# Hybrid attention, retention and state-space kernel on one core: mixers as parallel tasks, retention products ordered by shape, attention sums accumulated onto the scores

## The chip, the cores and the metric

The kernel runs on one core of a Trainium2 chip. The metric is the device time of one execution in microseconds (us). The core's engines are named as the profile names them: PE (TensorE, matrix products), PEld (its weight loads), DVE (VectorE), ACT (ScalarE), POOL (GpSimd) and SP (SyncE, which issues the DMAs here). Each engine takes its instructions in the order in which the built program lists them.

## The reference

Two layers over 528 positions (16 meta tokens and 512 inputs) of width 1024. Each layer projects the normed input to 23 blocks of 128 columns, feeds three mixers, multiplies their joined output by `w_out`, adds it to the stream, and ends with a gated MLP of width 2816. The three mixers:

```python
# stick-breaking attention, 6 heads, per block of 128 queries
z = einsum('bhqd,bhkd->bhqk', qb, kb) * scale
log1m = where(mask, log_sigmoid(-z), 0.0)
between = cumsum(log1m, axis=3, reverse=True) - log1m
w = where(mask, exp(log_sigmoid(z) + between), 0.0)
out = einsum('bhqk,bhkd->bhqd', w, vb)
# retention, 6 heads, chunks of 128: inside the chunk, and a state carried between chunks
scores = einsum('bhnid,bhnjd->bhnij', qc, kc) * decay_in
inner = einsum('bhnij,bhnje->bhnie', scores, vc)
o = inner + cross            # cross: the decayed state times q
# state space (S5): 16 groups, a complex diagonal recurrence, gelu, a gated product
```

## The kernel before

All matrix work in the large products is done as three products of split operands: a float is cut into a high part and a low part, and high times high, low times high and high times low are summed in PSUM (`mm3`, line 346). So each weight block needs a split on ACT (`wh`) and on DVE or POOL (`wl`), and each mixer output needs one too (`slow_split`, line 365: ACT writes `hi`, DVE or POOL writes `lo`). Products of 264 columns come in twos, since 528 positions fill two PSUM banks. The tiles `pj` are the results of the projections, of the gated product of S5, of the out product and of the MLP.

**How the order is made.** The program is written by a recorder. The projections are written one after the other, and between the products of `mm3` the function `tick` (line 183) lets waiting tasks write one step each. A task is a Python generator; `spawn` (line 166) adds it, and it goes on when its modelled time has come and what it asked for is there. Tasks share 5 PSUM banks (`banks`, `freed`, lines 177 and 180) and 7 attention groups. `drain` (line 200) writes tasks with no projection between them until a condition holds. The framework below then sorts the instructions of each engine once more by its own modelled times, keeping the dependencies. What reaches the chip is a fixed order for each engine.

**The mixers in the order before.** In each layer four lanes run beside the projections: two attention lanes (`sb_lane`, line 1094, one for each head of a pair, over three pairs), one retention lane (`ret_lane`, line 1105, three pairs one after the other) and one S5 lane (`s5_lane`, line 1112), which waits for both halves of `u`, runs `s5_mix` (line 702) over half 0 and then half 1, and then `s5_glu` (line 790). After the projections the out product is written in three parts (line 1142), each behind a `drain` for its mixers: attention, S5, retention in the first layer, and S5, attention, retention in the second.

**One attention group** (`sb_group`, line 816). Scores go into a bank `z` (products `z<-sq,sk`, with a mask product ahead of them in two of three groups). ACT makes log(1+exp(-|z|)) in tile `e` with three passes. DVE writes the softplus `sp` = max(z,0)+`e` and the log sigmoid `e` = min(z,0)-`e`, and the bank is given back. DVE then adds to `sp` the `sp` of the next block of keys, so that each block holds the running sum of all later ones. `sp` is split into `hi` (ACT) and `lo` (POOL). A second bank `s` takes the sums: products with `tri` (strict triangle) within a block and with `tric` (its complement) for the next block, 18 products with `tri` or `tric` for each head. DVE adds `s` to `e`, ACT takes the exponential, and the weights are split once more and multiplied with the values (`av`). Each head has three groups: A (432 columns), B2 (416) and B1 (512).

**One retention pair** (`ret_pair`, line 942). Transposes (`rtp`), a product for the states (`kv`), scores (`sc`) and then the output `ro`: for each of five chunks two products of 64 output rows, one per head, and one of 128 output rows with the state.

Of the kernel before, what the change touches and what calls it, by code (L numbers as in the profile page):

```python
# [9 lines left out]
F32R = mybir.dt.float32r  # L10
# [5 lines left out]
P = 128  # L16
# [20 lines left out]
Q = 4  # L37
# [51 lines left out]
def hybrid_kernel(ctx, tc, A, out, dbg=None):  # L89
# [137 lines left out]
    for name, g in (("A", G_A), ("B2", G_B2)):  # L227
# [3 lines left out]
        for j, q0, q1, o0 in g:  # L231
# [3 lines left out]
            if j == 4:  # L235
# [11 lines left out]
                    compare_op=ALU.is_gt, fill=0.0)  # L247
    G.affine_select(out=tri_f[:, P:2 * P], in_=tri_f[:, P:2 * P], pattern=[[1, P]], base=0, channel_multiplier=-1,
# [3 lines left out]
    tric = const([P, P], F32R, "tric")  # L252
    V.tensor_copy(out=tric, in_=tri_f[:, P:2 * P])
# [448 lines left out]
    def s5_mix(l, u, par, ys):  # L702
# [3 lines left out]
        for hf in range(2):  # L706
            ut = u[hf]
            uc = tt("uc")
            for t in range(4):
                for j in range(Q):  # L710
                    (SC.copy if (t + j) % 2 else V.tensor_copy)(
                        out=n3(uc)[32 * (3 - j):32 * (3 - j) + 32, t, :],
                        in_=ut[32 * t:32 * t + 32, :].rearrange("p (n q) -> p n q", q=Q)[:, :, j])
                yield
            pr, pi = ph[hf]
            fr, fi, y1, y2 = tt("fr"), tt("fi"), tt("y1"), tt("y2")
            for b in range(2):
                yield from banks(2)
                es = []
                for ri in range(2):  # L720
                    ps = bank("es")
                    for t in range(2):
                        mm(ps[:, NCH * t:NCH * t + NCH], lhsT=we[ri, hf][:, P * (2 * b + t):P * (2 * b + t) + P],
                           rhs=n3(uc)[:, 2 * b + t, :], start=True, stop=True)
                    es.append(ps)
                yield
                c = slice(HALF * b, HALF * b + HALF)
                er, ei = es[0][:, :HALF], es[1][:, :HALF]
                V.tensor_tensor(out=fr[:, c], in0=er, in1=pr[:, c], op=ALU.mult)
                V.tensor_tensor(out=y1[:, c], in0=ei, in1=pi[:, c], op=ALU.mult)  # L730
                V.tensor_tensor(out=fi[:, c], in0=ei, in1=pr[:, c], op=ALU.mult)
                V.tensor_tensor(out=y2[:, c], in0=er, in1=pi[:, c], op=ALU.mult)
                yield
                freed(2)
                G.tensor_tensor(out=fr[:, c], in0=fr[:, c], in1=y1[:, c], op=ALU.add)
                G.tensor_tensor(out=fi[:, c], in0=fi[:, c], in1=y2[:, c], op=ALU.subtract)
            yield
            for t in range(4):
                d0 = rho[:, 4 * hf + t:4 * hf + t + 1].to_broadcast([P, NCH])
                for z in (fr, fi):  # L740
                    V.tensor_tensor_scan(n3(z)[:, t, :], d0, n3(z)[:, t, :], 0.0, op0=ALU.mult, op1=ALU.add)
                if t % 2:
                    yield
            xr, xi, y2 = tt("xr"), tt("xi"), tt("y2")
            V.tensor_tensor(out=xr, in0=fr, in1=pr, op=ALU.mult)
            V.tensor_tensor(out=y1, in0=fi, in1=pi, op=ALU.mult)
            yield
            G.tensor_tensor(out=xr, in0=xr, in1=y1, op=ALU.subtract)
            V.tensor_tensor(out=xi, in0=fr, in1=pi, op=ALU.mult)
            V.tensor_tensor(out=y2, in0=fi, in1=pr, op=ALU.mult)  # L750
            yield
            G.tensor_tensor(out=xi, in0=xi, in1=y2, op=ALU.add)
            yield
            y = tt("ysm")
            for b in range(2):
                yield from banks(1)
                ps = bank("yps")
                for t in range(2):
                    o, tq = NCH * t, 2 * b + t
                    mm(ps[:, o:o + NCH], lhsT=tz[hf][:, P * tq:P * tq + P], rhs=n3(uc)[:, tq, :], start=True, stop=False)  # L760
                    for ri, x in ((0, xr), (1, xi)):
                        mm(ps[:, o + 1:o + NCH], lhsT=gg[ri, hf][:, 160 * tq + 32:160 * tq + 160],
                           rhs=n3(x)[:, tq, 0:NCH - 1], start=False, stop=ri == 1)
                yield
                for t in range(2):
                    tq = 2 * b + t
                    for i in range(Q):
                        V.scalar_tensor_tensor(
# [3 lines left out]
                            in1=ps[32 * i:32 * i + 32, NCH * t:NCH * t + NCH], op0=ALU.mult, op1=ALU.add)  # L772
                    yield
                freed(1)
            dump(f"ys{l}{hf}", y)

            y3 = tt("y3")
            SC.activation(y3, y, AF.Square)
# [505 lines left out]
```

## Time and profile before

| what | value |
|---|---|
| median of 3 runs | 1407.82 us (1406.98 to 1408.22) |
| the profiled execution | 1408.06 us, its span 1406.3 us |
| granted TensorE clock, mean over the span | 0.983 |
| PE busy | 97% of the span, 9020 products |
| DVE, ACT, POOL busy | 62%, 44%, 36% |
| DMA | 118.26 MB, mean 84 GB/s |

How to read the views. *Page, busy time*: an engine's busy us, share of the span, instructions. *Page, chain*: the work that ended last, followed back; shares of the span by engine. *Windows*: a stretch in us from the span's start, its length, then the busy us of PE, PEld, DVE, ACT and POOL, each with its instruction count, then the granted TensorE clock as a share of full speed (1.00 is 2.4 GHz, 0.50 is 1.2 GHz), the DMA share and GB/s; a window of PE alone has PE's busy time, the clock and the DMA columns. *Waits*: who waited for whom, us in total, times, longest. *Timeline*: start, duration, engine, line, operation, tiles, shape, count of merged instructions, and in brackets the idle time ahead and what ended it. *Lines*: group, shapes, count, then busy us and mean ns of one, then the idle time ahead. Products overlap in PE's pipeline: what one takes of PE is the distance from its start to the next start, not its duration. A float32 product (`ro`, `sc`, `kv`, `z`, `hps`) shows as two instructions in the trace.

### The profile page before, as it was taken

Reading aid. Unit: us, or ns where it says so; the run is one execution under the profiler, and the core shown is the slowest. Engines: PE = TensorE matmul, PEld = TensorE weight load, DVE = VectorE, ACT = ScalarE, POOL = GpSimd, SP = SyncE. Lnnn points to the kernel's source line nnn. Section 1 sums busy time; section 2 is a strip of 40 time slices with the busy share of each in tenths; the row PEclk is TensorE's granted clock in tenths of the full one; section 3 lists DMA queues with packets and bytes.
Section 4 is the critical chain, followed back from the end, with each engine's and each line's share of the span. In section 5 each row is a group of like instructions: output and inputs, shape, how many; then the busy total and the mean of one; then the engine's idle time right before and its main releaser. Section 6 shows DMA issues by size and latency. Waiting matters only on the chain. (4 is left out here: it accounts for less than half of the span.)

```text
span 1406.3 us, 22614 instructions
## 1 busy us (share of the span) xinstructions
PE 1362.0 (97%) x9020; PEld 1241.9 (88%) x9020; DVE 878.0 (62%) x1456; ACT 617.3 (44%) x1002; POOL 512.8 (36%) x625
## 2 busy tenths in 40 slices
PE   6999998899999999999999999999999999999998
PEld 6989888799989999999999898989788888888886
DVE  8897888768454645544556788774585543554453
ACT  4466475355343223322344565773363432442231
POOL 5686536322589402200223452653222210220020
PEclk9999899799999999999999999999999999999999
DMA  4212112113312222232232121222232322323223
GB/s 153 69 61 97 46 61 83 51 34 109 110 64 76 91 90 91 91 91 91 79 99 94 61 77 46 70 68 81 78 106 90 103 93 90 105 91 100 95 75 105
DMA packets 38985, 118.26 MB, mean 84 GB/s; under 512 B 4960, under 2 KB 5472, under 8 KB 38880
## 3 DMA queue, kind: packets, MB, share of 16 engines
q1 hardware_dynamic: 38880, 116.82, 25.6%
q8 instruction: 71, 1.16, 0.3%
q14 instruction: 34, 0.28, 0.1%
HBM read 111.46 MB, written 2.10 MB: 81 GB/s over the span
## 5 line engine op out<-in xcount | busy, mean ns | idle before, releaser
L131 PE MATMUL pj<-xh,wh 128*128 128x264 f32 (+1 forms) x1792 | 459.0, 312 | 16.7 <-ACT wh L121 5.3
L131 PE MATMUL pj<-xh,wl 128*128 128x264 f32 (+1 forms) x1792 | 456.3, 310 | 3.5 <-DVE wl L121 3.5
L131 PE MATMUL pj<-xl,wh 128*128 128x264 f32 (+1 forms) x1792 | 456.7, 311 | 1.8 <-DVE xl L121 1.8
L121 ACT CAST wh<-wr 128x1024 fp32r<-128x1024 f32 (+3 forms) x209 | 205.6, 986 | 411.7 <-PE pj L131 382.0
L131 PEld LDWEIGHTS pj<-xh,wh 128*128 128x128 f32 x1792 | 302.7, 192 | 36.0 <-ACT wh L121 5.3
L131 PEld LDWEIGHTS pj<-xh,wl 128*128 128x128 f32 x1792 | 302.2, 191 | 20.3 <-DVE wl L121 3.7
L131 PEld LDWEIGHTS pj<-xl,wh 128*128 128x128 f32 x1792 | 302.3, 191 | 19.6 <-DVE xl L121 2.5
L121 DVE TENSOR_TENSOR wl<-wr,wh 128x1024 fp32r<-128x1024 f32 (+3 forms) x166 | 252.1, 1520 | 75.1 <-ACT wh L121 72.6
L131 PE MATMUL pj<-lo,wh 128*128 128x264 f32 (+1 forms) x720 | 193.7, 322 | 0.0
L131 PE MATMUL pj<-hi,wl 128*128 128x264 f32 (+1 forms) x720 | 193.5, 322 | 0.1
L131 PE MATMUL pj<-hi,wh 128*128 128x264 f32 (+1 forms) x720 | 193.6, 323 | 0.0
L121 POOL TENSOR_TENSOR up<-ga,up 128x528 f32<-128x528 f32 (+1 forms) x44 | 61.8, 1405 | 347.2 <-DVE up L121 347.1
L121 DVE TENSOR_TENSOR h<-h,pj 128x264 f32<-128x264 f32 (+1 forms) x144 | 69.2, 510 | 140.1 <-PE pj L131 139.9
L121 POOL TENSOR_TENSOR wl<-wr,wh 128x1024 fp32r<-128x1024 f32 (+2 forms) x43 | 96.0, 2233 | 158.7 <-ACT wh L121 146.7
L131 PEld LDWEIGHTS pj<-hi,wh 128*128 128x128 f32 x720 | 120.4, 189 | 10.9 <-ACT wh L121 0.6
L131 PEld LDWEIGHTS pj<-hi,wl 128*128 128x128 f32 x720 | 120.3, 189 | 10.9 <-DVE wl L121 0.5
L131 PEld LDWEIGHTS pj<-lo,wh 128*128 128x128 f32 x720 | 120.4, 189 | 10.5 <-issue 0.3
L121 POOL TENSOR_TENSOR lo<-ga,hi 128x528 fp32r<-128x528 f32 (+1 forms) x44 | 59.0, 1340 | 158.7 <-ACT hi L121 158.6
L121 DVE TENSOR_TENSOR up<-pj,R 128x264 f32<-128x264 f32 (+1 forms) x66 | 32.1, 514 | 96.6 <-PE pj L131 96.6
L121 DVE TENSOR_TENSOR ga<-si,up 128x528 f32<-128x528 f32 (+1 forms) x44 | 31.7, 720 | 72.4 <-ACT si L121 58.4
L121 ACT ACTIVATE si<-si,bias 128x528 f32<-128x528 f32 (+1 forms) x44 | 32.1, 730 | 94.5 <-DVE si L121 94.5
L121 POOL TENSOR_TENSOR lo<-sp,hi 128x432 fp32r<-128x432 f32 (+2 forms) x36 | 46.6, 1305 | 36.4 <-ACT hi L121 34.0
(232 smaller groups left out, 1762.2 us busy)
## 6 DMA issues: line engine op xcount, KB each, us to landing
wr<-in_w_in_dram SPq DMA_DIRECT2D x45, 512.0 KB, 3.5
wr<-in_w_gate_dram SPq DMA_DIRECT2D x44, 512.0 KB, 3.5
wr<-in_w_up_dram SPq DMA_DIRECT2D x44, 512.0 KB, 3.4
wr<-in_w_down_dram SPq DMA_DIRECT2D x32, 512.0 KB, 3.4
wr<-in_w_out_dram SPq DMA_DIRECT2D x16, 384.0 KB, 3.1
wr<-in_w_down_dram SPq DMA_DIRECT2D x16, 384.0 KB, 3.1
rc<-in_rope_dram SPq DMA_DIRECT2D x12, 264.0 KB, 4.1
rs<-in_rope_dram SPq DMA_DIRECT2D x12, 264.0 KB, 4.8
```

The source lines that it names most:

```text
L121: return f(*a, **k)
L131: nc.tensor.matmul(out, lhsT=lhsT, rhs=rhs, start=start, stop=stop)
```

## The change

Four things are done.

1. Each retention pair gets a lane of its own (`ret_lane(p)`), and each half of S5 runs as a task of its own, spawned when its half of `u` is there.
2. In `ret_pair` the ten products of 64 output rows are written first, and the four of 128 output rows after them, with a step between.
3. In `sb_group` the sums are accumulated onto the scores in the bank `z` itself, with no second bank. The log sigmoid is not formed: log sigmoid(z) is z minus the softplus, and `tri` now holds the diagonal as well. DVE's running sums over blocks are gone: instead a product with `ones` (all -1) is made for each pair of a block and any later block.
4. The bank `z` is held until the exponential has read it.

```diff
-    def mm(out, lhsT, rhs, start, stop):
+    def mm(out, lhsT, rhs, start, stop, more=False):
...
-        nc.tensor.matmul(out, lhsT=lhsT, rhs=rhs, start=start, stop=stop)
+        nc.tensor.matmul(out, lhsT=lhsT, rhs=rhs, start=start, stop=stop, skip_group_check=more)
...
-    def s5_mix(l, u, par, ys):
+    def s5_mix(l, hf, ut, par, ys):
...
-        for hf in range(2):
-            ut = u[hf]
...
-            ys.append(y)
+        ys[hf] = y
...
         for j, q0, q1, o0 in g:
             mm(zp[:, o0:o0 + q1 - q0], lhsT=k[r, KT0[j]:KT0[j] + P], rhs=q[r, q0:q1],
-               start=m is None, stop=m is None or j == g[-1][0])
+               start=m is None and j == g[0][0], stop=j == g[-1][0], more=m is None)
...
-        s, m_ = tt("sp"), e
+        s = tt("sp")
         V.scalar_tensor_tensor(out=s[:, :n], in0=z, scalar=0.0, in1=e[:, :n], op0=ALU.max, op1=ALU.add)
-        V.scalar_tensor_tensor(out=m_[:, :n], in0=z, scalar=0.0, in1=e[:, :n], op0=ALU.min, op1=ALU.subtract)
+        yield
+        hl[gi] = yield from slow_split(s, n, G)
+
+        for part in range(2):
+            mm(zp[:, :n], lhsT=tri, rhs=hl[gi][part][:, :n], start=False, stop=True, more=True)
+        behind = [(j, q0, q1, o0, i) for j, q0, q1, o0 in g for i in place if i > j]
+        if any(place[t[4]][0] not in hl for t in behind):
+            yield lambda: all(place[t[4]][0] in hl for t in behind)
+        for j, q0, q1, o0, i in behind:
+            g1, o1, p0 = place[i]
+            a = max(q0, p0)
+            for part in range(2):
+                mm(zp[:, o0 + a - q0:o0 + q1 - q0], lhsT=ones, rhs=hl[g1][part][:, o1 + a - p0:o1 + q1 - p0],
+                   start=False, stop=True, more=True)
+        yield
+        SC.activation(e[:, :n], z, AF.Exp)
         yield
         freed(1)
-        yield lambda: all(j + 1 in where or j + 1 not in js or j + 1 in [t[0] for t in g] for j, *_ in g)
-
-        for j, q0, q1, o0 in reversed(g):
-            where[j] = (s, gi, o0, q0)
-            if j + 1 in where:
-                s1, _, o1, p0 = where[j + 1]
-                c = slice(o0 + max(q0, p0) - q0, o0 + q1 - q0)
-                V.tensor_tensor(out=s[:, c], in0=s[:, c], in1=s1[:, o1 + max(q0, p0) - p0:o1 + q1 - p0], op=ALU.add)
...
-        mm(sps[:, :n], lhsT=tri, rhs=hl[gi][0][:, :n], start=True, stop=False)
-        for j, q0, q1, o0 in g:
-            if j + 1 in js:
-                _, g1, o1, p0 = where[j + 1]
-                for part in range(2):
-                    mm(sps[:, o0 + max(q0, p0) - q0:o0 + q1 - q0], lhsT=tric,
-                       rhs=hl[g1][part][:, o1 + max(q0, p0) - p0:o1 + q1 - p0], start=False, stop=False)
-        mm(sps[:, :n], lhsT=tri, rhs=hl[gi][1][:, :n], start=False, stop=True)
-        yield
-        V.tensor_tensor(out=m_[:, :n], in0=m_[:, :n], in1=sps[:, :n], op=ALU.add)
-        yield
-        freed(1)
-        SC.activation(m_[:, :n], m_[:, :n], AF.Exp)
-        ws[gi] = yield from slow_split(m_, n, G)
+        ws[gi] = yield from slow_split(e, n, G)
...
-        for j in range(5):
...
-            if j:
-                mm(d, lhsT=st[:, P * (j - 1):P * j], rhs=q[:, P * j:P * j + n], start=False, stop=True)
-            if j == 2:
-                yield
+        for j, n, d in tiles:
             for hh in range(2):
...
+                mm(d[64 * hh:64 * hh + 64], lhsT=v[:n, P * j + 64 * hh:P * j + 64 * hh + 64],
+                   rhs=scs[hh][:n, P * j:P * j + n], start=j in (0, 4), stop=True, more=True)
+        yield
+        for j, n, d in tiles[1:]:
+            mm(d, lhsT=st[:, P * (j - 1):P * j], rhs=q[:, P * j:P * j + n], start=False, stop=True, more=True)
...
-            ys, so = [], []
-            yield from s5_mix(l, [got["u", 0], got["u", 1]], par[0], ys)
-            yield from s5_glu(l, ys, so)
+            ys, so = {}, []
+            spawn(s5_mix(l, 0, got["u", 0], par[0], ys), now[0][1])
+            yield lambda: ("u", 1) in got
+            spawn(s5_mix(l, 1, got["u", 1], par[0], ys), now[0][1])
+            yield lambda: len(ys) == 2
+            yield from s5_glu(l, [ys[0], ys[1]], so)
...
-        spawn(ret_lane())
+        for p in range(3):
+            spawn(ret_lane(p))
```

**What it moves, on DVE: the first attention groups of layer 0.** (`sp` is the softplus, `z` the score bank, `e` the log term, `sq` a projection result being scaled, `wl` a weight's low part.) Before:

```order
L121 SCALAR_TENSOR_TENSOR sp_1152<-z_1051,e_1090 128x432
L121 SCALAR_TENSOR_TENSOR e_1090<-z_1051,e_1090 128x432
L121 TENSOR_TENSOR sp_1152<-sp_1152 128x16
L121 TENSOR_TENSOR sp_1152<-sp_1152 128x144
L121 TENSOR_TENSOR sq_1161<-pj_970,R_144 128x264
L121 SCALAR_TENSOR_TENSOR sp_1174<-z_1056,e_1094 128x416
```

Now:

```order
L121 SCALAR_TENSOR_TENSOR sp_1151<-z_1050,e_1089 128x432
L121 TENSOR_TENSOR sq_1159<-pj_969,R_143 128x264
L121 SCALAR_TENSOR_TENSOR sp_1172<-z_1055,e_1093 128x416
L121 TENSOR_TENSOR sq_1159<-pj_970,R_143 128x264
L121 TENSOR_TENSOR wl_1192<-wr_967,wh_1191 128x1024
```

One instruction of DVE is left of each group, and what stood behind the others (here a projection's scaling and a weight split) moves up.

**On PE: the output products of the last retention pair of layer 0.** (`sc` are its scores, `rv` its values, `rm` the rotated queries, `st` the state.) Before, rows from the middle of the twelve that end it:

```order
L131 MATMUL ro_3616<-sc_3560,rv_3421 64x128
L131 MATMUL ro_3616<-sc_3583,rv_3421 64x128
L131 MATMUL ro_3616<-rm_2938,st_3510 128x128
L131 MATMUL ro_3616<-sc_3560,rv_3421 64x128
L131 MATMUL ro_3616<-sc_3583,rv_3421 64x128
L131 MATMUL ro_3616<-rm_2938,st_3510 128x128
```

Now, the last six rows:

```order
L132 MATMUL ro_3524<-sc_3499,rv_3378 64x128
L132 MATMUL ro_3524<-sc_3466,rv_3378 64x128
L132 MATMUL ro_3524<-sc_3499,rv_3378 64x128
L132 MATMUL ro_3525<-sc_3499,rv_3378 64x16
L132 MATMUL ro_3524<-rm_3034,st_3435 128x128 x3
L132 MATMUL ro_3525<-rm_3034,st_3435 128x16
```

Within a pair the shape of the product changes once instead of seven times.

**On PE: the end of the projections of layer 0.** (`pj<-xh` are products of the projections, `pj<-hi_1892` products of the out part behind them; `hps` is a norm's mean, `av` the weights times the values.) Before, the last projection product stands 32 rows ahead of these, and the first product of the out part four rows behind them:

```order
L131 MATMUL ro_3262<-sc_3204,rv_2956 64x16
L131 MATMUL ro_3262<-rm_2404,st_3096 128x16
L131 MATMUL hps_3297<-hsq_3288,blk 128x264
L131 MATMUL hps_3299<-hsq_3288,blk 128x264
L131 MATMUL av_3302<-hi_3251,v_1897 128x256
L131 MATMUL av_3302<-lo_3252,v_1897 128x256
```

Now:

```order
L132 MATMUL z_3028<-lo_3131,ones 128x16
L132 MATMUL ro_3219<-rm_2506,st_3020 128x128 x3
L132 MATMUL ro_3220<-rm_2506,st_3020 128x16
L132 MATMUL hps_3286<-hsq_3093,blk 128x264
L132 MATMUL hps_3288<-hsq_3093,blk 128x264
L132 MATMUL pj_3175<-xl_195,wh_2895 128x264
L132 MATMUL pj_3175<-xh_194,wl_2896 128x264
L132 MATMUL pj_3175<-xh_199,wh_2895 128x264
```

Eight projection products now stand behind those two `hps`, ahead of the next pair's `hps` and of `av`.

Counted in projection products of layer 0, S5's gated product starts some 160 earlier than before, now ahead of the end of the projections. The first retention pair's output products start some 160 later, the second pair's stand where they stood, at the end of the projections, and the third pair's some 60 earlier.

## Rows read from the trace of the kernel before

**Rows 1.** Page: busy time of PE, and the chain by engine.
```profile
PE 1362.0 (97%) x9020; PEld 1241.9 (88%) x9020; DVE 878.0 (62%) x1456; ACT 617.3 (44%) x1002; POOL 512.8 (36%) x625
...
PE 40%; DVE 0%; ACT 0%; issue 0%; POOL 0%; DVEq 0%; POOLq 0%
```

**Rows 2.** Windows: start, mixers of layer 0, its MLP, mixers of layer 1, MLP.
```profile
0.00:45.00 45.00, 31.48 (x198) 30.04 (x199) 35.27 (x106) 20.54 (x34) 21.73 (x46) 0.92 0.45 149
45.00:322.00 277.00, 261.96 (x1879) 241.61 (x1878) 228.72 (x481) 152.69 (x293) 151.28 (x194) 0.94 0.20 62
322.00:752.00 430.00, 425.64 (x3462) 424.36 (x3462) 227.39 (x308) 155.48 (x206) 159.07 (x259) 0.99 0.28 90
752.00:1020.00 268.00, 260.40 (x1834) 236.18 (x1833) 191.32 (x363) 153.41 (x293) 115.12 (x79) 0.99 0.22 71
1020.00:1406.30 386.30, 382.55 (x1655) 309.69 (x1653) 195.29 (x202) 135.19 (x177) 65.64 (x48) 1.00 0.29 96
```

**Rows 3.** Windows of PE alone: the disturbed stretches among layer 0's mixers.
```profile
147.00:152.50 5.50, 2.66 (x15) 0.89 0.00 0
152.50:165.00 12.50, 12.50 (x45) 0.50 0.15 44
242.50:250.20 7.70, 3.71 (x18) 0.78 0.01 2
264.00:269.00 5.00, 1.56 (x12) 0.83 0.13 27
269.00:282.50 13.50, 11.51 (x51) 0.56 0.09 31
```

**Rows 4.** Waits of PE from 45 to 322 us, the longest.
```profile
PE pj L131 <- ACT kt L121: 4.0, 1, 4.0
PE ro L131 <- DVE ysm L121: 2.4, 2, 2.0
PE s L131 <- ACT hi L121: 1.5, 1, 1.5
PE ro L131 <- DVE e L121: 1.2, 1, 1.2
```

**Rows 5.** Timeline of DVE and of ACT ahead of the wait of 4.0 us.
```profile
242.88 1.47 DVE L121 TENSOR_TENSOR rsw<-rsw,rs 128x528 f32<-128x528 f32 x1 [2.86 <-DMA rsw<-rq]
...
244.61 0.55 ACT L121 CAST hi<-sp 128x432 fp32r<-128x432 f32 x1 [3.13 <-DVE sp L121]
```

**Rows 6.** Lines of DVE from 45 to 322 us: the instructions that go.
```profile
L121 DVE TENSOR_TENSOR sp<-sp 128x16 f32<-128x16 f32 (+2 forms) x30 | 11.8, 400 | 0.2
L121 DVE SCALAR_TENSOR_TENSOR e<-z,e 128x432 f32<-128x432 f32 (+2 forms) x18 | 11.1, 616 | 0.0
L121 DVE TENSOR_TENSOR e<-e,s 128x432 f32<-128x432 f32 (+2 forms) x18 | 11.0, 617 | 0.2
...
L121 DVE TENSOR_TENSOR sp<-sp,sp 128x256 f32<-128x256 f32 x6 | 5.0, 835 | 0.1
```

**Rows 7.** Timeline of PE: products with `tric` at full clock.
```profile
254.50 0.23 PE L131 MATMUL s<-hi,tric 128*128 128x144 f32 x1
...
254.86 0.44 PE L131 MATMUL s<-lo,tri 128*128 128x432 f32 x1
...
261.49 0.28 PE L131 MATMUL s<-hi,tric 128*128 128x256 f32 x1
...
261.73 0.39 PE L131 MATMUL s<-lo,tri 128*128 128x512 f32 x1
```

**Rows 8.** Timeline of PE: a retention pair's output products, and eight products of one shape.
```profile
967.74 0.44 PE L131 MATMUL ro<-sc,rv 128*64 128x128 f32 x4
968.11 0.49 PE L131 MATMUL ro<-rm,st 128*128 128x128 f32 x2
968.53 0.44 PE L131 MATMUL ro<-sc,rv 128*64 128x128 f32 x4
...
253.17 1.05 PE L131 MATMUL kv<-rv,kt 128*128 128x128 f32 x8
```

More of the change, by code (lines that the diff above doesn't have):

```diff
@@ new lines, in s5_mix @@
+        uc = tt("uc")
+        for t in range(4):
+            for j in range(Q):
+                (SC.copy if (t + j) % 2 else V.tensor_copy)(
+                    out=n3(uc)[32 * (3 - j):32 * (3 - j) + 32, t, :],
+                    in_=ut[32 * t:32 * t + 32, :].rearrange("p (n q) -> p n q", q=Q)[:, :, j])
+            yield
+        pr, pi = ph[hf]
+        fr, fi, y1, y2 = tt("fr"), tt("fi"), tt("y1"), tt("y2")
+        for b in range(2):
+            yield from banks(2)
+            es = []
+            for ri in range(2):
+                ps = bank("es")
+                for t in range(2):
+                    mm(ps[:, NCH * t:NCH * t + NCH], lhsT=we[ri, hf][:, P * (2 * b + t):P * (2 * b + t) + P],
+                       rhs=n3(uc)[:, 2 * b + t, :], start=True, stop=True)
+                es.append(ps)
+            yield
+            c = slice(HALF * b, HALF * b + HALF)
+            er, ei = es[0][:, :HALF], es[1][:, :HALF]
+            V.tensor_tensor(out=fr[:, c], in0=er, in1=pr[:, c], op=ALU.mult)
+            V.tensor_tensor(out=y1[:, c], in0=ei, in1=pi[:, c], op=ALU.mult)
+            V.tensor_tensor(out=fi[:, c], in0=ei, in1=pr[:, c], op=ALU.mult)
+            V.tensor_tensor(out=y2[:, c], in0=er, in1=pi[:, c], op=ALU.mult)
+            yield
+            freed(2)
+            G.tensor_tensor(out=fr[:, c], in0=fr[:, c], in1=y1[:, c], op=ALU.add)
+            G.tensor_tensor(out=fi[:, c], in0=fi[:, c], in1=y2[:, c], op=ALU.subtract)
@@ new lines, in s5_mix @@
+        yield
+        for t in range(4):
+            d0 = rho[:, 4 * hf + t:4 * hf + t + 1].to_broadcast([P, NCH])
+            for z in (fr, fi):
+                V.tensor_tensor_scan(n3(z)[:, t, :], d0, n3(z)[:, t, :], 0.0, op0=ALU.mult, op1=ALU.add)
+            if t % 2:
+                yield
+        xr, xi, y2 = tt("xr"), tt("xi"), tt("y2")
+        V.tensor_tensor(out=xr, in0=fr, in1=pr, op=ALU.mult)
+        V.tensor_tensor(out=y1, in0=fi, in1=pi, op=ALU.mult)
+        yield
+        G.tensor_tensor(out=xr, in0=xr, in1=y1, op=ALU.subtract)
@@ new lines, in s5_mix @@
+        dump(f"ys{l}{hf}", y)
+        y3 = tt("y3")
+        SC.activation(y3, y, AF.Square)
+        yield
+        V.tensor_scalar(out=y3, in0=y3, scalar1=0.044715, scalar2=1.0, op0=ALU.mult, op1=ALU.add)
+        V.tensor_tensor(out=y3, in0=y3, in1=y, op=ALU.mult)
+        V.tensor_scalar(out=y3, in0=y3, scalar1=-25.0, scalar2=None, op0=ALU.max)
+        yield
+        sigmoid(y3, y3, 2.0 * math.sqrt(2.0 / math.pi))
+        yield
+        V.tensor_tensor(out=y, in0=y, in1=y3, op=ALU.mult)
@@ L813, in s5_glu, with sb_group @@
             yield
-    def sb_group(q, k, r, g, gi, js, where, hl, ws):
+    def sb_group(q, k, r, g, gi, place, hl, ws):
         n = width(g)
```

142 lines of the change are left out of this document (41 added, 101 removed).

## The prediction

> **What bounds the kernel now.** I read the page first, for who is busy, then the windows by stage, then PE's waits and the timeline around the longest, and last the prices of the instructions that change.
>
> The page says that PE is busy for 1362.0 of 1406.3 us, and that no other engine holds a share of the chain that ended last [rows 1]. So the time is PE's work, plus what PE loses. It loses in two ways: it stands idle, or it works at the lower of its two clock levels. The windows show where [rows 2]. In the MLP of layer 1 (1020 us on) the clock is 1.00, and only 3.8 us are idle. Among the mixers of layer 0 (45 to 322 us) PE is idle for 277.0 - 262.0 = 15.0 us, and the granted clock is 0.94. Among the mixers of layer 1 it is idle for 268.0 - 260.4 = 7.6 us at 0.99. The same mixers run in both; what differs is DVE, which is busy for 228.7/277 = 83% in layer 0 and 191.3/268 = 71% in layer 1.
>
> The loss of layer 0 sits in three places [rows 3]. After an idle stretch the clock falls to 0.50, and a stretch with no idle time at all follows at half speed: from 152.5 to 165.0 PE is busy throughout at 0.50. Busy time times the missing clock is what this costs: 12.5 x 0.50 = 6.2 us there, 11.5 x 0.44 = 5.1 from 269, and 3.7 x 0.22 = 0.8 from 242.5. That is 12 us beside the 15 idle: a loss of 27 us in layer 0. In layer 1 it is 7.6 idle and 268 x 0.01 = 2.7 at most, so 10.
>
> Who makes PE wait? The longest waits name ACT and DVE [rows 4]. The wait of 4.0 us is put down to ACT, but ACT itself stood 3.13 us for DVE, and DVE stood 2.86 us at a multiply that waited for a DMA (the rotation's swapped copy), with the running sums of attention queued behind it [rows 5]. DVE takes its instructions in order, so a late one holds back everything behind it, weight splits included.
>
> **The change, part by part.** The sum is made against the profiled execution of 1408.06 us, 0.2 us from the median. A difference of about 0.2%, 2.8 us, is what a measurement of this kernel can tell from none.
>
> *Sums over blocks on PE instead of DVE: added.* Before, a head has 12 products with `tric`; now it has 26 with `ones`: three pairs of blocks in group A and ten in B1 and B2, each with a high and a low part. The 14 that are new have 256 columns (2), 144 (4) and 16 (8). Four products of 144 and 16 columns take 254.86 - 254.50 = 0.36 us of PE, 0.09 each, and two of 256 columns 261.73 - 261.49 = 0.24, 0.12 each [rows 7]. So a head costs 2 x 0.12 + 12 x 0.09 = 1.3 us more, and twelve heads **+15.8 us**. These are PE's own time; nothing hides them. In the Trainium skill, "TensorE: Matmul & The Clock Gate", section "Back-to-back issue gap", a lone product is spaced by its columns, with a floor of about 25 ns up to 64 columns; by that estimate the new products cost 8.0 us, and the sum below would be 1391. The row is of the same products with a weight load ahead of each, so the row decides.
>
> *Retention by shape: removed.* A chunk repeats every 968.53 - 967.74 = 0.79 us: 0.37 for four instructions of 64 rows and 0.42 for two of 128 rows [rows 8]. Eight `kv` of one shape take 1.05 us with the last one's 0.28 tail, so 0.11 each [rows 8]. At that pace two instructions of 128 rows cost 0.22, and four of 64 rows, which start in twos, also 0.22. So a change of shape costs 0.20 one way and 0.15 the other. Six of seven go in each pair: 3 x 0.20 + 3 x 0.15 = 1.05 us, for six pairs **-6.3 us**. The bounds are 0, if the shapes are not what is paid for, and 6 x 1.4 = -8.4, if the instructions of 64 rows reach 0.05 each.
>
> *Nothing for ACT and POOL.* Passes and splits of a group are the same in number. The mask products, scores and `tri` products are the same too. The weight of the gated product (one DMA) is moved behind some twenty others on SP's queue; None of PE's longest waits names a DMA [rows 4], so I cost it nothing. If it came late, S5's out part would stand, which comes second in layer 0 and has the retention tail behind it.
>
> *DVE's work removed.* In layer 0 the 18 log sigmoids, 18 last sums and 36 running sums go: 11.1 + 11.0 + 11.8 + 5.0 = 38.9 us [rows 6]; layer 1 has the same instructions. None of it is on PE, so its worth is only in PE's loss. DVE's load in layer 0 falls to 228.7 - 38.9 = 190 us, or 71% if the stage shrinks by some 10 us: just the load that layer 1 has now, at a loss of 10 us [rows 2]. I take that loss as the likely one: idle from 15.0 to 7.6 and the half clock from 12 to 2.7, **-16.7 us**. Layer 1's own loss of 10 us falls less, since part of its waits are for DMAs and ends of chains: **-2**. The bounds are 0 (DVE was not what was late) and -30 (nearly all 37 us go).
>
> *The tasks in parallel.* They add no instruction. The order shows S5's gated product ahead of the end of layer 0's projections, and eight projection products between steps at that end, where the trace has its third loss (264 to 282.5, 3.4 us idle, then 2.0 more and half clock) [rows 3]. That is how the -16.7 could be had in this place. What is late next is the chain of a group behind its last sum: exponential and split on ACT, low part on POOL, then `av`.
>
> Sum: 15.8 - 6.3 - 16.7 - 2 = -9.2, so 1408.1 - 9.2 = **1399 us**.
>
> **The rivals.**
>
> *PE is full, and its losses stay.* The 4.0 us wait began with a DMA that DVE waited for [rows 5], and removing sums does not make it land earlier. If waits like that make up the loss, only the work counts: 1408.1 + 15.8 - 6.3 = **1418**, slower. The place is 45 to 322 us, and the point from which this decides is a loss in both mixer stages above 37 - 9.5 = 27 us. For it: DVE idles within the wait. Against: the load differs by 12 points between the layers, and the loss by 17 us. The Trainium skill, "Perfetto Trace Analysis", section "Identifying the Most-Contended Engine", says to optimize the engine of highest occupancy first; by that rule, work moved from DVE at 62% onto PE at 97% makes the kernel slower. Chance 0.22.
>
> *The score bank, held longer, starves the others.* A bank is now held through split, sums and exponential, and all tasks share five. If two more stretches like the one from 147 to 165 appear (2.8 idle and 6.2 of clock each), it is 1418 + 18 = **1436**. Against: the order puts no gap there, and the second bank of the group is gone. Chance 0.06.
>
> *Half the relief.* Loss falls by 9.5 us only: 1408, no difference. Chance 0.14.
>
> *The whole loss goes.* -30 in place of -18.7: **1388**. For it: the third place has its cover in the new order. Chance 0.13.
>
> *It does less than it says:* the framework sorts again, so the parallel tasks need not run earlier. The order shows the first retention pair later and the second unmoved; the term does not rest on them. This is inside the half case.
>
> **How the numbers follow.** The forecast has 0.45. Faster takes it and the whole relief: 0.58. Same is the half case: 0.14. Slower is the full PE and the starved banks: 0.28. The range goes from 1386, two below the whole relief, to 1418, the full PE; it leaves out the starved banks, half of the full PE's spread and a part of the whole relief's, about 0.2. Faster cases hold most of it: the forecast's own range, by the bounds of the shapes and of the idle time, is 1391 to 1405.
>
> **What would show it.** PE should have 168 products more, and DVE 144 instructions less and some 80 us less busy time. A `ro` chunk should cost near 0.44 us in place of 0.79, and `ones` products 0.09 to 0.12 us apart. From 45 us to the end of layer 0's mixers PE should be idle for 7 to 8 us at a clock near 0.99, with DVE near 71%. The forecast is wrong if idle and clock loss there stay near 27 us, or if the new products stand further apart than those in the rows.

## The result, and the profile of the changed kernel

The changed kernel takes 1417.2 us (median of 6 runs, 1413.7 to 1421.8), the kernel before 1406.7 beside it (6 runs, 1405.1 to 1408.2). The ratio is 1.0077, with an interval from 1.0056 to 1.0098: slower by some 11 us, where 9 us faster was forecast. The profiled execution took 1416.61 us, its span is 1414.9.

The page, busy time and chain by engine [rows 1]:

```profile
PE 1367.1 (97%) x9188; PEld 1253.7 (89%) x9188; DVE 807.3 (57%) x1312; ACT 619.3 (44%) x1002; POOL 509.2 (36%) x624
...
PE 84%; DVE 9%; POOL 3%; ACT 2%; issue 1%; DMA 0%; SPq 0%; DVEq 0%; ACTq 0%
```

The work moved as forecast: PE has 168 products more, DVE 144 instructions and 878.0 - 807.3 = 70.7 us of busy time less (some 80 were forecast). PE's share has not changed. The chain is followed over nearly the whole span here and runs through DVE for 9% of it. That of before can't be set beside it: its shares add up to 40% [rows 1], so it was followed over the last part of the span alone.

The windows by stage [rows 2]: start, mixers of layer 0, its MLP, mixers of layer 1, MLP.

```profile
0.00:45.00 45.00, 31.33 (x197) 29.87 (x198) 34.95 (x106) 20.63 (x34) 22.65 (x45) 0.92 0.45 149
45.00:322.00 277.00, 262.12 (x1967) 246.26 (x1966) 191.73 (x409) 153.27 (x293) 152.06 (x194) 0.97 0.20 62
322.00:751.00 429.00, 424.05 (x3463) 422.78 (x3463) 226.36 (x309) 155.49 (x206) 158.81 (x259) 0.99 0.28 90
751.00:1028.30 277.30, 266.81 (x1917) 245.25 (x1916) 159.20 (x290) 154.68 (x293) 110.02 (x79) 0.99 0.21 68
1028.30:1414.90 386.60, 382.81 (x1654) 309.59 (x1652) 195.10 (x202) 135.27 (x177) 65.68 (x48) 1.00 0.29 96
```

Three of the five stages stand within 1 us of before. The mixers of layer 0 take 277 us again, the mixers of layer 1 take 277.3 in place of 268. DVE's load fell in both, to 191.7/277 = 69% and 159.2/277.3 = 57%. But PE's idle time is 14.9 us in layer 0, as before, and in layer 1 it rose from 7.6 to 277.3 - 266.8 = 10.5. PE's longest waits are new ones [rows 4]; first 45 to 322 us, then 740 to 1030:

```profile
PE rtp L138 <- DVE rm L121: 7.4, 1, 7.4
PE z L132 <- POOL lo L121: 1.9, 2, 1.1
PE z L132 <- ACT hi L121: 1.8, 1, 1.8
...
PE vps L138 <- DVE sv L121: 3.4, 1, 3.4
PE pj L132 <- DVE rk L121: 2.7, 1, 2.7
PE hps L132 <- ACT hsq L121: 1.9, 2, 1.3
```

The 4.0 us wait of before is gone. In its place PE stands 7.4 us at the transposes of the third retention pair, and 3.4 and 2.7 us at the start of layer 1, for DVE. The disturbed stretches of PE alone [rows 3]:

```profile
275.50:283.20 7.70, 0.31 (x4) 0.63 0.26 69
283.20:288.00 4.80, 4.80 (x24) 0.52 0.01 3
288.00:296.00 8.00, 8.00 (x66) 1.00 0.09 27
```

The wait of 7.4 us is this idle stretch. Behind it PE is busy throughout, but the granted clock is 0.52 for 4.8 us, and 1.00 from there on. What DVE did there, from its timeline [rows 5]:

```profile
273.29 1.94 DVE L121 TENSOR_TENSOR wl<-wr,wh 128x768 fp32r<-128x768 f32 x1 [11.27 <-ACT wh L121]
...
275.83 0.75 DVE L121 SCALAR_TENSOR_TENSOR rk<-rk,cols,hsq 128x528 f32<-128x528 f32 x1
...
279.05 0.41 DVE L121 TENSOR_TENSOR sbo<-avl,av 64x256 f32<-64x256 f32 x1
280.58 0.71 DVE L121 TENSOR_TENSOR rsw<-rsw,rs 128x528 f32<-128x528 f32 x1 [1.12 <-DMA rsw<-rk]
281.40 1.61 DVE L121 TENSOR_TENSOR rm<-rm,rsw 128x528 f32<-128x528 f32 x1
```

The rotated k of the pair waits for its swapped copy, a DMA, as the rotated q did ahead of the old wait, and the transposes of that pair now stand ahead of the out part's products in PE's order. It is no queue of DVE's work: DVE itself had stood idle for 11.27 us up to 273.29, and again for 1.12 us for the DMA.

### The profile page after: what moved, and what is told of

Its sections match the earlier page's. It is cut to its first block, busy times and chain, and to the rows that moved or that the text cites. A ratio compares the mean times of both kernels' runs of the same rounds, so it can differ in the third digit from the quotient of the medians.

```text
span 1414.9 us, 22768 instructions
## 1 busy us (share of the span) xinstructions
PE 1367.1 (97%) x9188; PEld 1253.7 (89%) x9188; DVE 807.3 (57%) x1312; ACT 619.3 (44%) x1002; POOL 509.2 (36%) x624
## 3 DMA queue, kind: packets, MB, share of 16 engines
q1 hardware_dynamic: 38880, 116.82, 25.4%
## 4 chain that ended last, share of the span: by engine, by line
PE 84%; DVE 9%; POOL 3%; ACT 2%; issue 1%; DMA 0%; SPq 0%; DVEq 0%; ACTq 0%
PE pj L132 72%; PE z L132 5%; DVE ysm L121 2%; PE hps L132 2%; PE av L132 1%; PE ro L132 1%; PE sc L132 1%; DVE y L121 1%; DVE s5w L121 1%; DVE wl L121 1%; DVE fr L121 1%; POOL st L121 1%; PE kps L132 1%; PE rtp L138 0%; PE kv L132 0%
## 5 line engine op out<-in xcount | busy, mean ns | idle before, releaser
L132 PEld LDWEIGHTS pj<-xl,wh 128*128 128x128 f32 x1792 | 300.2, 192 | 20.5 <-DVE xl L121 2.9
L121 ACT ACTIVATE e<-z 128x416 f32<-128x416 f32 (+2 forms) x72 | 38.7, 547 | 44.3 <-PE z L132 43.6
```

The costliest lines, as they stand in the source:

```text
L121: return f(*a, **k)
```

## The experiments

All times are medians. The kernel before ran beside them and took 1408.3 us (beside e1 to e4), 1407.4 (e5 to e8), 1408.1 (e9 to e12) and 1407.1 (e13 to e16). Three theories went in. Work theory: only PE's instructions count, its losses stay. Relief theory: the prediction's own. Placement theory: the parallel tasks put work where it collides.

### One part of the change at a time

**e1_shape**: before, with the retention's output products by shape.

```
+ for j, n, d in tiles:          # ten products of 64 rows
+     for hh in range(2): mm(d[64 * hh:...], v..., scs[hh]...)
+ yield
+ for j, n, d in tiles[1:]:      # four of 128 rows
+     mm(d, st..., q...)
```

> The kernel before with the retention products ordered by shape and nothing else changed. Work theory (only PE's instructions count, its losses stay): 6 x 1.05 us less, about 1400.5. Placement theory (the parallel tasks are what costs): the same 1400.5, since no task is moved. Relief theory (the prediction's own): the same. If it stays at 1406 to 1408, the changes of shape are not what was paid for; if it comes out above 1408, reordering alone moves the waits by several us.

Measured: 1410.8 us (11 runs), ratio 1.0017 [1.0007, 1.0027]. It is slower by 2 us, so all theories missed, and only the sentence on reordering fits.

**e2_tasks**: before, with `s5_mix` spawned once for each half and `ret_lane` once for each pair.

```
- yield lambda: ("u", 1) in got and bool(par)
+ yield lambda: ("u", 0) in got and bool(par)
- yield from s5_mix(l, [got["u", 0], got["u", 1]], par[0], ys)
+ spawn(s5_mix(l, 0, got["u", 0], par[0], ys), now[0][1])
+ yield lambda: ("u", 1) in got
+ spawn(s5_mix(l, 1, got["u", 1], par[0], ys), now[0][1])
- spawn(ret_lane())
+ for p in range(3): spawn(ret_lane(p))
```

> The kernel before with the retention pairs and the halves of the state space as parallel tasks, nothing else. Work theory: no instruction is added, 1407, within 2 us. Placement theory: 5 to 10 us slower, 1412 to 1417, with the loss in layer 1, where both halves of the state space then load DVE at once, and PE waiting for DVE there for over 5 us more than before. Relief theory: 0 to 4 us faster, by the cover at the end of layer 0's projections.

Measured: 1417.3 us, ratio 1.0059 [1.0045, 1.0073]. The tasks alone cost 9 us and add no instruction. The time is the placement theory's, and so is the layer: PE's idle time among the mixers of layer 1 goes from 7.6 to 14.2 us. But the waits of PE there that name DVE grow by 2.1 us only, from 5.4 to 7.5, and not by over 5; the longest, 4.1 us, names POOL.

**e3_sums**: before, with the attention sums on the scores (the `sb_group` of the change, `ones` in place of `tric`).

> The kernel before with the attention sums accumulated onto the scores, nothing else. Work theory: 15.8 us slower, about 1422.5, with the idle time and clock of both mixer stages as before. Relief theory: 15.8 - 18.7, about 1404, and the idle time of layer 0's mixers falls from 15 us to about 8. Placement theory: between, about 1410 to 1415, since DVE's relief pays in layer 0 where no task was moved.

Measured: 1396.1 us, ratio 0.9905 [0.9890, 0.9919]. It is 12 us faster than before, better than the relief theory said, and against both others. The mixers of layer 0 and of layer 1 in windows:

```profile
45.00:312.60 267.60, 262.48 (x1944) 244.09 (x1943) 187.36 (x408) 151.65 (x290) 149.37 (x194) 0.97 0.21 64
742.50:1009.50 267.00, 265.42 (x1917) 243.52 (x1916) 158.74 (x290) 153.49 (x293) 112.47 (x79) 1.00 0.23 71
```

Idle time is 5.1 us in layer 0 and 1.6 in layer 1, where before it was 15.0 and 7.6 [rows 2]. DVE's load is the changed kernel's within 5 us (187.4 and 191.7 in layer 0). So nearly the same load goes with an idle time of 5.1 here and 14.9 there: the load alone does not tell it.

**e4_shape_tasks**: shapes and tasks, sums as before.

> The changed kernel with the attention sums as they were: retention by shape and parallel tasks alone. Work theory: 1400.5, the 16 us of the new products gone. Placement theory: 1406 to 1411, what the shapes give being lost again. Relief theory: 1398 to 1401, and slower than the whole change by nothing to 3 us less; the changed kernel's 1417 then speaks against it already.

Measured: 1413.3 us, ratio 1.0039 [1.0027, 1.0052]. Above the placement theory's range by 2 us, far above the others.

### The parts beside the sums

**e5_shape_sums**: the changed kernel without the tasks.

> The changed kernel without the parallel tasks: attention sums and retention by shape. If the tasks alone are what costs, it stands at about 1396, where the sums alone stood, or 4 to 6 us below (1390), if the shapes pay; the idle time of both mixer stages is then as with the sums alone (about 5 us in layer 0, below 2 in layer 1). If each reordering moves the waits anew (luck of the order), it lies anywhere between 1392 and 1405. If the tasks are not to blame, it stays above 1410.

Measured: 1408.7 us (12 runs, from 1397.9 to 1414.4), ratio 1.0005 [0.9987, 1.0024]. The shapes, which take products together, cost 12.5 us here. This is outside the range given to the luck of the order, and the runs spread widely.

**e6_sums_s5**: the sums, and the state space's halves as tasks (the `s5` part of e2's edit).

> The sums alone (1396 us) with the two halves of the state space as parallel tasks. Crowding theory (both halves at the start of layer 1 load DVE at once): about 10 us slower than 1396, 1404 to 1408, with PE's waits for DVE between 775 and 815 us back (3.4 us at the transposes of v behind sv). If the retention lanes are to blame, it stays at 1396 within 2 us.

Measured: 1417.7 us, ratio 1.0073 [1.0055, 1.0090]. The halves cost 1417.7 - 1396.1 = 21.6 us, twice what was expected, and give the changed kernel's time by themselves, though without its wait of 7.4 us.

**e7_sums_ret**: the sums, and the retention pairs as tasks (the `ret` part of e2's edit).

> The sums alone (1396 us) with the retention pairs as parallel tasks. If the early transposes of the third pair (7.4 us of idle in the changed kernel at 283 us) are the lanes' own doing, it is 6 to 8 us slower, about 1403, with that stall in it; if that stall comes with the state space's halves only, it stays at 1396 within 2 us.

Measured: 1400.3 us (11 runs, 1396.1 to 1407.7), ratio 0.9951 [0.9933, 0.9968]. Four us are lost, less than expected, and the 7.4 us wait is not in it: its longest wait among the mixers of layer 0 behind 200 us is 1.1 us. It is in neither e6 nor e7, so beside the sums it takes the lanes and the overlapping halves together.

**e8_sums_load**: the sums, with DVE's old work put back, written into a tile that nobody reads.

```
  V.scalar_tensor_tensor(out=s[:, :n], ...)
+ V.scalar_tensor_tensor(out=junk[:, :n], in0=z, ..., op0=ALU.min, op1=ALU.subtract)
+ for j, q0, q1, o0 in reversed(g):
+     if j + 1 in place: V.tensor_tensor(out=junk[:, c], in0=s[:, c], in1=s[:, c], op=ALU.add)
...
+ V.tensor_tensor(out=junk[:, :n], in0=s[:, :n], in1=z, op=ALU.add)
  SC.activation(e[:, :n], z, AF.Exp)
```

> The sums alone (1396 us) with DVE's removed work put back as a load that nobody waits for: the log sigmoid, the running sums and the last sum of each group are computed by DVE with their old widths into a tile that is not read. PE's instructions are those of the sums alone. Load theory (DVE's load makes PE wait): the relief goes again, 1396 + 12 to 17, so 1408 to 1413, and more than before the change, since PE's new products stay; idle time of both mixer stages back to 15 and 7 us. Chain theory (the relief is the shorter chain of a group: two DVE passes and a second bank fewer between its scores and its weights): it stays within 4 us of 1396.

Measured: 1427.7 us, ratio 1.0149 [1.0136, 1.0163]: 31.5 us above the sums alone, with the same number of products on PE, and above both ranges expected. Its windows:

```profile
45.00:332.10 287.10, 271.87 (x1957) 253.13 (x1956) 222.98 (x478) 152.53 (x292) 148.52 (x194) 0.94 0.19 60
760.50:1033.40 272.90, 266.90 (x1916) 243.94 (x1915) 199.72 (x362) 153.59 (x293) 111.42 (x79) 1.00 0.22 69
```

Idle time in layer 0 is 15.2 us at a clock of 0.94: the loss of before [rows 2]. In layer 1 it is 6.0, before 7.6. But the work does not stand where nobody waits for it. ACT's waits, of e8 and then of before:

```profile
ACT e L121 <- DVE junk L121: 54.4, 21, 8.7
...
ACT e L121 <- DVE e L121: 22.6, 13, 4.5
```

All 21 are exponentials of a group that start when the last `junk` of that group ends, as 13 of before started when DVE's last sum ended. So e8 puts back DVE's load and a step of the group's chain with it. It shows that the sums pay by taking this work off DVE; whether by the load or by the shorter chain, it does not tell.

### The order kept

The break between two steps of the retention task moved with the shapes, from behind eight products to behind ten, and with it the order of everything after it. These two keep it at eight; against e1:

```
  for j, n, d in tiles:
      for hh in range(2): mm(...)
+     if j == 3: yield
- yield
```

**e9_shape_same_order**: before with this. DVE, ACT and POOL have exactly the order of before.

> The kernel before with the retention products ordered by shape, but with the break between two steps of the task behind eight products, as before, and not behind ten. Then DVE, ACT and POOL have the very order of before, and PE differs in the ro products alone. If the gain of the shapes (0.88 us a pair in the traces, 5.3 us in all) was eaten by the new order of everything else, it is 1402 to 1403, against 1410.8 of the same products with the break moved. If the shapes give nothing on the path, it is 1407.

Measured: 1403.0 us (9 runs), ratio 0.9964 [0.9952, 0.9976]: 5.1 us faster, as expected. The 24 instructions of a pair (12 products) that stand together, in the timeline of before (first product, and the one behind the last), of e9 and of the changed kernel [rows 8]:

```profile
966.74 0.65 PE L131 MATMUL ro<-sc,rv 128*64 128x128 f32 x6
...
969.78 0.36 PE L131 MATMUL pj<-xh,wl 128*128 128x264 f32 x1
```

```profile
961.00 1.30 PE L132 MATMUL ro<-sc,rv 128*64 128x128 f32 x16
962.23 1.06 PE L132 MATMUL ro<-rm,st 128*128 128x128 f32 x8
963.14 0.37 PE L132 MATMUL pj<-xh,wl 128*128 128x264 f32 x1
```

```profile
299.16 1.30 PE L132 MATMUL ro<-sc,rv 128*64 128x128 f32 x16
300.39 1.06 PE L132 MATMUL ro<-rm,st 128*128 128x128 f32 x8
301.30 0.49 PE L132 MATMUL pj<-hi,wh 128*128 128x264 f32 x2
```

From the first product to the next work it is 969.78 - 966.74 = 3.04 us before, 963.14 - 961.00 = 2.14 in e9 and 301.30 - 299.16 = 2.14 in the changed kernel. So this pair saves 0.90 us, and six like it would save 5.4.

**e10_sums_shape_same_order**: the sums with it.

> The sums alone (1396 us) with the retention products by shape and the break where it was. Order theory: 1396 - 5.3, about 1391, the fastest so far. If the sums' new order has no room for it or is unstable, 1396 to 1408, like the version with the break moved (1408.7, from 1398 to 1414).

Measured: 1394.8 us, ratio 0.9904 [0.9882, 0.9925]. 14 us below the version with the break moved, but only 1.3 below the sums alone, not 5. The order kept its worth, the shapes did not; why, no run here tells. The order is not quite that of e3 either: in the traces DVE's differs at 4 places and ACT's at 6.

### The halves held apart

**e11_sums_s5_held**: e6, with the second half not started until the first is done.

```
- yield lambda: ("u", 1) in got
+ yield lambda: ("u", 1) in got and 0 in ys
```

> The sums alone with the two halves of the state space as tasks, but the second half held until the first is done, so that only the early start is left and not the overlap (1417.7 us with the overlap, 1396 without the tasks). If the overlap costs (both halves on DVE at once), it comes back to 1396 to 1400, and PE's waits of 3.4 and 2.5 us between 780 and 812 us are gone. If the early start is to blame, it stays above 1410. Luck of the order: anywhere between.

Measured: 1397.2 us, ratio 0.9926 [0.9908, 0.9944]. Of the 21.6 us, 20.5 are gone. It is the overlap that costs, not the early start.

**e12_after_mended**: the whole change, with this line and with the break behind eight.

> The whole change with two mends: the second half of the state space is held until the first is done, and the break in the retention products lies behind eight. Overlap theory: the 10 us of layer 1 come back, and the retention lanes cost their 4: 1396 - 5.3 + 4, about 1395. If the 7.4 us wait at the third pair's transposes in layer 0 belongs to the lanes, it stays and the time is 1400 to 1403. If neither mend matters, 1417.

Measured: 1387.9 us, ratio 0.9859 [0.9838, 0.9881]. It is faster than either theory said.

**e13_after_held**: the whole change, with this one line.

> The whole change with the second half of the state space held until the first is done, and the break in the retention products as in the change (behind ten). If the overlap is what took the relief back: 1388 to 1393, some 25 us below the change. If the break is the larger part, above 1405.

Measured: 1386.5 us, ratio 0.9851 [0.9830, 0.9871]: below every value expected. One line takes 30.7 us off the changed kernel, and this is the lowest time of all, though e12 is within the noise of it. Its windows over the mixers of both layers:

```profile
45.00:304.60 259.60, 254.85 (x1948) 239.75 (x1948) 186.72 (x408) 151.57 (x290) 151.90 (x194) 0.99 0.21 66
732.70:999.10 266.40, 263.93 (x1916) 243.88 (x1915) 162.83 (x290) 153.52 (x293) 116.29 (x79) 1.00 0.23 71
```

Layer 0 takes 17.4 us less than in the changed kernel, layer 1 takes 10.9 less. Idle time falls from 14.9 to 4.7 and from 10.5 to 2.5. PE's longest waits in the mixers of layer 1, and then in those of layer 0, are

```profile
PE av L132 <- POOL lo L121: 1.4, 1, 1.4
PE hps L132 <- ACT hsq L121: 1.0, 1, 1.0
...
PE pj L132 <- DVE py L121: 2.0, 1, 2.0
```

so all three long waits that name DVE are gone, the 7.4 us in layer 0 too, with the lanes still there. Where DVE's load of layer 1 went is seen in the first 60 us of that layer, in windows of 20 us; of the columns PE, PEld and DVE busy come first. The changed kernel:

```profile
751.00:771.00 20.00, 20.00 (x165) 19.73 (x164) 18.90 (x46) 12.19 (x23) 6.21 (x7) 1.00 0.21 72
771.00:791.00 20.00, 15.10 (x118) 14.26 (x117) 19.06 (x32) 5.13 (x10) 11.22 (x8) 1.00 0.16 54
791.00:811.00 20.00, 16.27 (x117) 14.52 (x116) 17.08 (x38) 11.35 (x22) 2.88 (x2) 1.00 0.08 27
```

With the half held, where the layer begins 18 us sooner after the start of the span, but 732 and 751 us are the same place in the work:

```profile
732.00:752.00 20.00, 20.00 (x165) 19.87 (x164) 15.93 (x36) 8.88 (x16) 6.83 (x7) 1.00 0.25 79
752.00:772.00 20.00, 19.95 (x144) 18.00 (x142) 17.22 (x34) 9.28 (x19) 6.48 (x3) 1.00 0.23 76
772.00:792.00 20.00, 20.00 (x158) 19.61 (x158) 9.25 (x20) 15.60 (x30) 9.70 (x6) 1.00 0.17 58
```

In the changed kernel DVE is busy for 55.0 of the 60 us, and PE stands idle for 8.6 of them. With the half held DVE comes to 42.4 of 60, and PE to 0.05 idle. The stage as a whole has the same DVE work in both (159.2 and 162.8 us): it is bunched, not more. The overlap is shown as the cause by e11 and e13; that it acts through DVE's bunched work in layer 1 is read from these windows and from the waits, which name DVE. The 3.4 us wait speaks for it too: it is in all six kernels whose halves overlap in layer 1 (the changed one, e2, e4, e6, e14 and e15), and in the twelve others it is 0.5 us or not there.

Layer 0 is another matter. Three of its stretches in the changed kernel:

```profile
145.00:165.00 20.00, 17.43 (x118) 16.40 (x118) 19.87 (x33) 11.30 (x23) 12.32 (x11) 0.91 0.23 68
165.00:185.00 20.00, 18.88 (x149) 17.85 (x149) 19.55 (x35) 8.66 (x19) 13.47 (x9) 1.00 0.08 27
265.00:285.00 20.00, 11.78 (x85) 10.73 (x82) 10.33 (x13) 12.03 (x24) 9.06 (x10) 0.81 0.10 27
```

In the first two, where the halves' mixing runs, DVE is full and PE is idle for 3.7 us. But 8.2 of the stage's 14.9 us of idle time lie in the third, where DVE is busy for half the time: that is the 7.4 us wait, read above as a matter of the transposes' place in PE's order. Holding the half takes it away by changing the order; why the order comes out so is not shown.

**e14_after_break**: the whole change, with the break behind eight only.

> The whole change with the break behind eight products, as in the kernel before, and the halves of the state space overlapping as in the change. Only PE's ro products then stand otherwise than in the change; DVE, ACT and POOL keep its order. If the overlap is what took the relief back: 1414 to 1419, the change's time. If the break matters in this order too, 1400 to 1410.

Measured: 1415.3 us, ratio 1.0060 [1.0039, 1.0081]. The 7.4 and 3.4 us waits are both in it. The break is not what made the change slow.

**e15_mended_overlap_1**: e12, with the halves overlapped in layer 1 alone.

```
- yield lambda: ("u", 1) in got and 0 in ys
+ yield lambda: ("u", 1) in got and (l == 1 or 0 in ys)
```

> The mended change (1387.9 us) with the halves of the state space overlapping again in layer 1 alone. By the traces (the sums alone against the sums with the halves overlapped: 11 us in layer 1, 6.5 in layer 0) about 11 us slower, 1399, with PE waiting for DVE between 775 and 815 us. If layer 0 was the place, 1388 to 1390.

Measured: 1400.3 us, ratio 0.9945 [0.9926, 0.9964]: 12.5 us slower than e12, and with the changed kernel's waits, 3.4 and 2.7 us, at the same instructions. The rest of the overlap's price, some 18 us of the 30.7 by subtraction, is then layer 0's; the windows of the changed kernel and of e13 differ there by 17.4.

**e16_mended_no_lanes**: e12, with the retention pairs in one lane.

> The mended change with the retention pairs in one lane, as before. If the lanes cost 4 us, as they did beside the sums alone, it is 1384. If they pay in this order, 1391 to 1396: the sums with the half held (1397.2) less the shapes' 5.3 is 1392.

Measured: 1391.8 us, ratio 0.9894 [0.9874, 0.9913]. The lanes pay 3.9 us here; beside the sums alone they cost 4.2.

## Why the prediction was wrong, step by step

**The step that failed** is "The tasks in parallel. They add no instruction." The sum gave them no price, and its text took them for a help at the end of layer 0's projections. Their overlap of the two halves costs 30.7 us in the changed kernel (1417.2 against 1386.5 with the halves held apart), and 20.5 beside the sums alone (e6 and e11). The line that holds the half moves other work too, and order alone moved the time by up to 14 us (e5 and e10), so the size of this price depends on the order; its sign was the same each time. No rival had this mechanism; the nearest, "It does less than it says", said that the term doesn't rest on the tasks. It did: in layer 0, 186.7 us of DVE's work go with 4.7 us of idle time with the halves in turn (e13), and 191.7 go with 14.9 without.

**The rule that led there** was to read PE's loss off DVE's mean load of a stage, "just the load that layer 1 has now, at a loss of 10 us". The changed kernel refutes it: 69% goes with an idle time of 14.9 us, and layer 1's 57% goes with 10.5, more than before's 71% with 7.6. The windows of 20 us, which the prediction does not use, show the danger for layer 1. In before, with one half at a time, DVE is busy for 75 to 82% of each of the first three in layer 1:

```profile
752.00:772.00 20.00, 19.95 (x162) 19.61 (x160) 15.16 (x29) 9.32 (x16) 6.25 (x4) 1.00 0.25 82
772.00:792.00 20.00, 19.46 (x136) 17.55 (x137) 14.93 (x28) 10.93 (x22) 6.91 (x5) 1.00 0.21 76
792.00:812.00 20.00, 18.53 (x133) 16.84 (x132) 16.41 (x29) 11.63 (x22) 11.78 (x8) 1.00 0.18 61
```

Of these 46.5 us, 11.2 are attention's sums, which the change takes away, so 60 - 46.5 + 11.2 = 24.7 us are free for what the second half brings. By DVE's timeline the mixing of both halves takes 50.5 us in this layer of before, so that one takes some 25: it would fill all that is free. In the changed kernel 45.4 us of mixing fall into these 60 us, in e13 27.2.

**Sums on PE, +15.8: right in kind, 2.5 us short.** The twenty products with `ones` of one head's groups B1 and B2, in the timeline of e3: the first, the first of 256 columns, and what follows the last:

```profile
938.11 0.23 PE L132 MATMUL z<-hi,ones 128*128 128x144 f32 x1
...
938.70 0.36 PE L132 MATMUL z<-hi,ones 128*128 128x256 f32 x1
...
940.29 1.14 PE L132 MATMUL kv<-rv,kt 128*128 128x128 f32 x8
```

Twenty products take 940.29 - 938.11 = 2.18 us, 0.109 each, so 168 take 18.3 us at that pace. A second measure is near: e8, with DVE's work put back, is 1427.7 - 1407.4 = 20.3 us above before. The spacing of a lone product in the Trainium skill ("TensorE: Matmul & The Clock Gate", section "Back-to-back issue gap"), by which it would have been 8.0, is not what this stream shows, as the prediction took it; the section itself says that in a stream with weight loads both instructions set the spacing.

**Relief of DVE, -16.7 and -2: too small, and then taken back.** With the sums alone the time is 12.2 us lower although PE has 18.3 us more to do, so the loss fell by 30.5; putting DVE's work back costs 31.5. The bound of -30 ("nearly all 37 us go") was the right value for this part. The order with the halves overlapped gave it away again.

**Shapes, -6.3: about right.** 5.4 us by the rows of e9, 5.1 by its time. But the break that moved with them changes the order elsewhere: with it the shapes cost 2.5 us instead of gaining 5.1 on their own, and 12.5 instead of gaining 1.3 beside the sums. The text counted every product and no break.

**The DMA of the gated product's weight, nothing: it stands.** None of PE's longest waits leads to it.

**The rivals.** "PE is full, and its losses stay" gave 1418, and the time is 1417.2. Its mark is met as well: idle time of 25.4 us in both stages, and with the missing clock (262.1 x 0.03 + 266.8 x 0.01) 36, above its 27. But its mechanism is refuted by e3: the losses do go when the sums leave DVE, and the old 4.0 us wait is gone. The loss in the changed kernel is a new one of nearly the same size (by the same count it was 15.0 + 7.6 + 262.0 x 0.06 + 260.4 x 0.01 = 41 before), so that this number fits to 1 us is luck. An estimate closes on it: 18.3 - 5.4 - 5 = 8 us slower, and the spans are 8.6 apart. Beside it the prediction set the rule that the engine of highest occupancy comes first (the Trainium skill, "Perfetto Trace Analysis", section "Identifying the Most-Contended Engine"; for PE the section goes by the arithmetic done and by the share of the weight loads, which is 88% here [rows 1]). What the prediction drew from it, that work moved onto PE makes the kernel slower, did not come true in e3: 18 us more on PE at 97% went with a time 12 us lower. "The score bank, held longer, starves the others" (1436) is refuted by e3 too, which holds it as long.

**Its own signs.** The 168 products more, the 144 instructions less and the pace of `ones` (0.109 us) came true. In layer 0 PE should have been idle for 7 to 8 us at a clock near 0.99, and was for 14.9 at 0.97. One reading was wrong from the start: "no other engine holds a share of the chain" rests on a row whose shares add up to 40%, so it tells nothing of the mixers of layer 0.

**What stays open.** Why the place of a break between two steps moves the time by 14 us beside the sums (e5 and e10), by 7.8 in before (e1 and e9), and hardly in the whole change, is not settled. In e1 no new long wait stands out; layer 1 loses it in several waits of 1 to 2 us. Nor is it settled whether the sums pay by DVE's lighter load or by a group's shorter chain. It was also not tried whether the overlap could be had without loss, with part of DVE's work on another engine.

## What to carry to other kernels

Work taken from an engine that the bound engine often waits for can be worth more than it costs, even when it lands on the bound engine. Putting the work back shows that in one run, but look at who waits for it there: a result that nobody reads can still hold up the next step. Before two equal pieces of work are made parallel, look at short windows in which the first one runs now, not at the stage's mean: what the engine that they share has free there, with what the change takes away from it, must hold the second, or the work queued behind both comes late. A change that consists of several parts should be taken apart first: here a part worth 12 us and one that cost 31 were both inside a difference of 11.

## What the runs showed of the hardware

An instruction of DVE with two inputs in SBUF took longer while POOL split a weight. In the changed kernel, ahead of the wait of 3.4 us, DVE and then POOL:

```profile
780.94 2.77 DVE L121 SCALAR_TENSOR_TENSOR sk<-sk,cols,hsq 128x528 f32<-128x528 f32 x1
783.64 0.42 DVE L121 TENSOR_TENSOR_SCAN fr<-rho,fr 128x132 f32<-128x132 f32 x1
783.98 0.74 DVE L121 TENSOR_TENSOR sv<-pj,R 128x264 f32<-128x264 f32 x2
```

```profile
780.69 2.46 POOL L121 TENSOR_TENSOR wl<-wr,wh 128x1024 fp32r<-128x1024 f32 x1
```

The multiply `sk` has 528 columns and takes 2.77 us; its like, `rk` at 275.83, takes 0.75 beside a `MEMSET` on POOL, which has no input. `sk` ends 0.56 us after POOL's split, which began 0.25 us before it. The Trainium skill, "SBUF — State Buffer", section "Who interferes with whom", says that a DVE instruction with two SBUF inputs contends with a GpSimd instruction that reads SBUF, and that the port pair they share is an exclusive lock; these rows agree. So, read this way, 2 of the 3.4 us of that wait go back to POOL's split, which stood in the way of DVE and not of PE. It is no part of what the change did: in before, `sq` of the same shape takes 2.74 us at 768.22, beside a split on POOL that takes 2.38 us from 768.02.

One more thing I did not expect: the sensitivity to order. The runs of e5 lie between 1397.9 and 1414.4 us, more apart than the changed kernel and the one before, while those of e13, which loses the least, lie within 1.3 us.
